# Where the state-space parameters keep their tables and operands: six tiles change their buffer pool, and one clearing is held back

## The chip, the cores and the metric

The program runs on one core of one Trainium2 chip (trn2). The metric is the device time of one execution in microseconds (us). The names used for the engines are PE (TensorE, matmul), PEld (its weight load), DVE (VectorE), ACT (ScalarE), POOL (GpSimd) and SP (SyncE, which here only issues DMAs).

## The reference

Four layers over 512 tokens of width 2048, in float32, and a norm behind the last. The first layer ("ab") is gated linear attention beside forgetting attention, the second ("c") a state-space layer, the third and fourth are a recurrent unit with window attention, and latent attention with differential attention. The change is in the parameters of the state-space layer, which depend on its weights alone. They are all that is shown:

```python
def s5_ssm(u, lam_re, lam_im, log_step, b_re, b_im, c_re, c_im, d):
    # groups of 16 channels share a 64-dim complex diagonal state:
    # x_t = Lbar x_(t-1) + Bbar u_t ; y_t = Re(C x_t) + D u_t
    lr = jnp.minimum(lam_re, -1e-4); li = lam_im
    step = jnp.exp(log_step)[:, None]
    mag = jnp.exp(lr * step)
    lb_re, lb_im = mag * jnp.cos(li * step), mag * jnp.sin(li * step)
    den = lr * lr + li * li
    nr, ni = lb_re - 1.0, lb_im
    coef_re = (nr * lr + ni * li) / den
    coef_im = (ni * lr - nr * li) / den
    bb_re = coef_re[..., None] * b_re - coef_im[..., None] * b_im
    bb_im = coef_re[..., None] * b_im + coef_im[..., None] * b_re
    ...                                   # scan over the tokens with Lbar, Bbar, C, D

def layer_c(x, ...):
    u, gate = split(rms_norm(x) @ w_in, 2)
    z = gelu(s5_ssm(u, ...))
    z = z * sigmoid(z @ glu_w + glu_b)
    return x + (z * silu(gate)) @ w_out
```

## The kernel before

Activations lie feature by feature: a tile is 128 features by 512 tokens. Every float32 factor of a large product is split into a high part and a rest (`split`: ACT rounds the high part, DVE subtracts it), and a product is three matmuls of 128x512 (high times high, high times rest, rest times high). Activations split this way are in tiles `hl`, weights in `whl`: a piece of weights comes by DMA into `wraw`, ACT writes its high part into `whl`, DVE the rest, and 12 matmuls then use it (`pj<-hl,whl` or `pj<-whl,hl`, all at line 152, where the one helper for matmuls stands; all two-operand elementwise work of DVE and POOL stands at line 140). There are four buffers of `whl` and three of `wraw`.

Tiles are taken from pools by tag (`self.t(tag, ...)`), with the number of buffers in `BUFS` (line 109): here `ha` 8, `hb` 3, `hc` 4, `vs` 4, `wk` 4, `wt` 2, `bc` 2, `rawa` 8, `rawb` 8; `cst`, `acc`, `acc2`, `fac` and `lm` have one. A new tile of a tag waits until the readers of the tile that had the buffer before are done. In PSUM, `pj` has four buffers, `sc` two, `tr` and `po` one each. A scheduler that simulates the program while it is built sets the order of the instructions in each engine's queue; on the chip each engine runs its queue strictly in that order and waits on semaphores. The order is thus fixed, and it depends on which buffer each tile has.

The parameters of layer c are worked out during layer ab and its output product, a piece at each of 21 places (`beside(o)` in the layer, `params(o)` in `emit`, o = 0 to 20):

- o = 0: `s5_params` (line 831), nearly all on POOL. It ends with two tables of powers, `Tb` (16 powers, 128x1024, two tiles of `vs`, lines 946 to 955) and `Ta` (8 powers, `hc`), and copies them by rows of four groups through `wt` into a table in device memory: 16 rows `s5tab` (lines 983 to 990), each by six copies on POOL and a DMA from POOL's queue. Before that a small table `s5w` goes out over `wrow` (`ha`, line 932).
- o = 1 to 8: `s5_tables(2(o-1))` (line 998) loads two rows of `s5tab` into `lm` and forms with DVE, for each of the two, a cosine and a sine table `C`, `Sn` of 128x512 (`hc`, line 1006), each from two products (`cst`, `acc`) and a sum. They go out by DMA (`s5ph`), issued by ACT's queue. I call one such cosine or sine table with its three DVE instructions a half-table; there are 32.
- o = 3 to 18: `s5_batch_params(o-3)` (line 1022), for batch b = 0 to 15: it loads `M`, `X1`, `Y` (two `vs` each), makes on POOL two outputs over `Z` (`cst`, line 1046) into `hc` and sends them out, on DVE the operand `GG` (`acc2`, line 1060) and on POOL the operand `BB` (`fac`, line 1072). At the next place follow PE's 32 small products of them (`tr<-vs,fac` and `tr<-acc,fac`, lines 1081 to 1086), and their result goes over `X3`, a part of `X1`, to device memory.

Layer ab in the stretch that matters: `fox(i)`, i = 0 to 3, is forgetting attention for two heads (scores `sc`, softmax by DVE and ACT, transposes into `tr`, copy to `pt`, products `po` with the value tiles, which lie in `vs`), and between them stand the projections of the next heads and the gates. The mixed output of the layer is in `rawa` and `rawb`, eight tiles each, `rawb` filling up from fox(0) to fox(3); `split_all` turns all sixteen into `hl` (`hl<-rawa,hl`, `hl<-rawb,hl`) at the start of `w_out`, the output product. Layer c later takes a tile `M0` per batch (`hb`, line 1099), cleared by POOL at line 1101; nothing there holds the clearing back until layer c.

## Time and profile before

| | |
|---|---|
| median of 3 runs | 3413.39 us (3410.92 to 3414.65) |
| the profiled execution | 3418.24 us, of which the span (first to last instruction) is 3416.4 us |
| PE busy | 3350.7 us, 98% of the span |
| DVE, ACT, POOL busy | 1907.5 us (56%), 1335.0 us (39%), 784.1 us (23%) |
| mean granted TensorE clock | 0.993 |

A row "`a<-b`" names the tile written and the tiles read, by the program's names. "[3.48 <-DVE whl L140]" behind a row of a timeline is the idle time of that engine just before it, and what ended it: the instruction of DVE at line 140 that wrote `whl`. PEclk is the TensorE clock that was granted in a stretch, as a share of full speed. Busy shares are means over the whole program; what counts for a change in one stage is who waits for whom in that stage.

### The profile page before, as it was taken

Reading aid. Unit: us, or ns where it says so; the run is one execution under the profiler, and the core shown is the slowest. Engines: PE = TensorE matmul, PEld = TensorE weight load, DVE = VectorE, ACT = ScalarE, POOL = GpSimd, SP = SyncE. Lnnn points to the kernel's source line nnn. Section 1 sums busy time; section 2 is a strip of 40 time slices with the busy share of each in tenths; the row PEclk is TensorE's granted clock in tenths of the full one; section 3 lists DMA queues with packets and bytes.
Section 4 is the critical chain, followed back from the end, with each engine's and each line's share of the span. In section 5 each row is a group of like instructions: output and inputs, shape, how many; then the busy total and the mean of one; then the engine's idle time right before and its main releaser. Section 6 shows DMA issues by size and latency. Waiting matters only on the chain.

```text
span 3416.4 us, 45778 instructions
## 1 busy us (share of the span) xinstructions
PE 3350.7 (98%) x16332; PEld 2719.7 (80%) x16332; DVE 1907.5 (56%) x3213; ACT 1335.0 (39%) x2497; POOL 784.1 (23%) x974
## 2 busy tenths in 40 slices
PE   8999998998999999999999999999999999999997
PEld 7888886776788888888888777888888788888885
DVE  5753457778455666834355656453544545647634
ACT  4442432233243333423343554232433444535522
POOL 0330365348612223300222010012110120212011
PEclk9999999999999999999999999999999999999999
DMA  5223335576634444343443223334333223232333
GB/s 149 75 69 90 89 99 168 165 217 196 203 121 131 137 144 136 119 120 119 144 127 90 71 72 87 96 120 142 107 90 83 72 65 83 79 90 73 107 118 107
DMA packets 389013, 390.01 MB, mean 114 GB/s; under 512 B 66968, under 2 KB 327448, under 8 KB 388784
## 3 DMA queue, kind: packets, MB, share of 16 engines
q1 hardware_dynamic: 362992, 354.64, 36.4%
q10 hardware_dynamic: 22464, 22.12, 1.9%
q0 software_dynamic: 3328, 10.32, 0.8%
q8 instruction: 128, 2.10, 0.3%
q14 instruction: 101, 0.83, 0.1%
HBM read 340.71 MB, written 46.25 MB: 113 GB/s over the span
## 4 chain that ended last, share of the span: by engine, by line
PE 89%; POOL 4%; DVE 3%; DMA 2%; issue 1%; ACT 1%; ACTq 0%; DVEq 0%; SPq 0%; POOLq 0%
PE pj L152 79%; PE sc L152 4%; PE po L152 3%; PE tr L156 2%; DMA s5tab<-wt 1%; POOL vs L140 1%; POOL hc L140 1%; PE tr L152 1%; POOL fac L140 1%; POOL cst L140 1%; POOL wt L140 0%; DVE whl L140 0%; DVE wk L140 0%; POOL wt L987 0%; POOL acc L140 0%
## 5 line engine op out<-in xcount | busy, mean ns | idle before, releaser
L152 PE MATMUL pj<-hl,whl 128*128 128x512 f32 x10224 | 2463.4, 398 | 16.8 <-DVE whl L140 8.8
L152 PEld LDWEIGHTS pj<-hl,whl 128*128 128x128 f32 x10224 | 1912.8, 189 | 462.6 <-DVE whl L140 11.4
L140 DVE TENSOR_TENSOR whl<-wraw,whl 128x512 fp32r<-128x512 f32 (+2 forms) x1064 | 806.3, 760 | 1091.4 <-ACT whl L137 1083.4
L137 ACT ACTIVATE whl<-wraw 128x512 fp32r<-128x512 f32 (+2 forms) x1064 | 661.1, 623 | 1367.0 <-PE pj L152 1098.1
L152 PE MATMUL pj<-whl,hl 128*128 128x512 f32 (+2 forms) x2112 | 463.5, 378 | 7.6 <-DVE ha L140 3.8
L152 PEld LDWEIGHTS pj<-whl,hl 128*128 128x128 f32 x2112 | 372.5, 189 | 84.9 <-DVE whl L140 4.6
L140 POOL TENSOR_TENSOR acc<-acc,wt 128x512 f32<-128x512 f32 x73 | 102.9, 1418 | 798.6 <-ACT wt L137 797.4
L137 ACT ACTIVATE wk<-sc,sm 128x256 f32<-128x256 f32 (+3 forms) x160 | 79.6, 501 | 90.1 <-DVE sm L148 86.6
L140 POOL TENSOR_TENSOR ha<-wk,ha 64x512 fp32r<-64x512 f32 x32 | 45.0, 1406 | 290.7 <-ACT ha L137 264.2
L140 POOL TENSOR_TENSOR wt<-wt,acc 64x508 f32<-64x508 f32 x32 | 63.8, 1994 | 181.5 <-DVE wt L140 125.8
L140 POOL TENSOR_TENSOR wt<-ha,wk 128x256 f32<-128x256 f32 x72 | 62.4, 894 | 133.0 <-PE pj L152 60.0
L152 PE MATMUL po<-pt,vs 128*128 128x128 f32 x560 | 79.9, 276 | 0.0
L152 PE MATMUL sc<-ha,ha 128*128 128x128 f32 (+1 forms) x224 | 71.7, 392 | 3.5 <-DVE ha L140 2.8
L152 PEld LDWEIGHTS po<-pt,vs 128*128 128x128 f32 x560 | 72.8, 192 | 2.8 <-ACT pt L137 0.4
L156 PE MATMUL tr<-ident,wk 128*128 128x128 f32 x416 | 71.4, 274 | 1.4 <-DVE pt L509 1.1
L137 ACT ACTIVATE pt<-tr 128x384 f32<-128x384 f32 (+3 forms) x96 | 46.7, 487 | 62.2 <-PE tr L156 60.3
L148 DVE TENSOR_SCALAR wk<-wk,sm 128x256 f32<-128x256 f32 (+3 forms) x160 | 65.0, 420 | 4.5
L156 PEld LDWEIGHTS tr<-ident,wk 128*128 128x128 f32 x416 | 52.0, 141 | 18.8 <-issue 3.4
L137 ACT ACTIVATE ge<-ge 128x512 f32<-128x512 f32 x64 | 40.3, 630 | 68.1 <-DVE ge L140 56.6
L140 POOL TENSOR_TENSOR fac<-wt,acc 128x512 fp32r<-128x512 f32 x8 | 10.8, 1352 | 244.2 <-ACT acc L137 130.4
L521 DVE TENSOR_REDUCE sm<-sc 128x1 f32<-128x128 f32 (+3 forms) x96 | 45.9, 487 | 34.1 <-PE sc L152 33.3
L140 POOL TENSOR_TENSOR cst<-vs,vs 128x256 f32<-128x256 f32 x64 | 54.0, 863 | 34.6 <-DMA vs<-s5w 27.2
(316 smaller groups left out, 2983.6 us busy)
## 6 DMA issues: line engine op xcount, KB each, us to landing
wraw<-in_l_w_in_dram SPq DMA_DIRECT2D x272, 256.0 KB, 2.8
wraw<-in_ab_w_in_dram SPq DMA_DIRECT2D x216, 256.0 KB, 2.8
wraw<-in_c_w_in_dram SPq DMA_DIRECT2D x128, 256.0 KB, 2.7
wraw<-in_l_w_out_dram SPq DMA_DIRECT2D x128, 256.0 KB, 2.9
wraw<-in_ab_w_out_dram SPq DMA_DIRECT2D x64, 256.0 KB, 3.3
wraw<-in_glu_w_dram SPq DMA_DIRECT2D x64, 256.0 KB, 3.0
wraw<-in_c_w_out_dram SPq DMA_DIRECT2D x64, 256.0 KB, 2.9
wraw<-in_l_w_in_dram SPq DMA_DIRECT2D x128, 128.0 KB, 2.3
```

The lines of the kernel that those rows point to most:

```text
L137: return self.nc.scalar.activation(out, in_, func, **kw)
L140: return (eng or self.nc.vector).tensor_tensor(out, a, b, op=op)
L148: return e.tensor_scalar(out, a, s1, None, op0=op0)
L152: return self.nc.tensor.matmul(out, l, r, start=start, stop=stop)
L156: return self.nc.tensor.transpose(out, in_, self.ident[:k, :k])
L521: self.nc.vector.tensor_reduce(mx, pb[:, 0:w], axis=AX.X, op=ALU.max)
```

## The change

- `wrow` goes from the pool `ha` into `lm`, which has one buffer.
- `Tb` goes from two tiles of `vs` into four halves in `rawb` (`Tb`, `Tb2`), so that a row of `s5tab` takes eight copies instead of six.
- `C` and `Sn` go from `hc` to `rawb`.
- `Z` goes from `cst` to `bc`.
- `GG` and `BB` of odd batches go to `hc`; those of even ones stay in `acc2` and `fac`.
- The clearing of `M0` is held behind the last instruction of that kind in the parameters (the clearing of `X3`, line 1087 before, 1090 after).

```diff
--- before.py
+++ after.py
@@ -929,7 +929,7 @@
                     s_ = 2 * half + j
                     o = (2 * i + j) * P
                     self.tr(pw_[0:64, o:o + P], N[8 + i] if s_ == 3 else W[:, i, s_])
-            wrow = self.t("ha", [64, 2, 2, P])
+            wrow = self.t("lm", [64, 2, 2, P])
             self.act(wrow.rearrange("p i j f -> p (i j f)"), pw_[0:64])
             for j in range(2):
                 for gg in range(2):
@@ -943,7 +943,8 @@
         cmul(c2, d2, co, si, co, si)
         cmul(N[11], N[12], c2, d2, c2, d2)
 
-        Tb = [self.t("vs", [P, 16, H]) for _ in range(2)]
+        half = lambda: self.hd("rawb").rearrange("p (n h) -> p n h", h=H)
+        Tb, Tb2 = [half(), half()], [half(), half()]
         Ta = [self.t("hc", [P, 8, H]) for _ in range(2)]
         tmp = [self.t(tag, [P, 8, H]) for tag in ("fac", "acc2")]
         tt_ = self.t("cst", [P, S])
@@ -960,12 +961,13 @@
 
                 pb_ = [p_.to_broadcast([P, m, H]) for p_ in pw]
                 u0, u1 = tmp[0][:, 0:m], tmp[1][:, 0:m]
+                to = Tb2 if m == 8 else [x[:, m:2 * m] for x in tab]
                 self.tt(u0, tab[0][:, 0:m], pb_[0], A.mult, eng=g)
                 self.tt(u1, tab[1][:, 0:m], pb_[1], A.mult, eng=g)
-                self.tt(tab[0][:, m:2 * m], u0, u1, A.subtract, eng=g)
+                self.tt(to[0], u0, u1, A.subtract, eng=g)
                 self.tt(u0, tab[0][:, 0:m], pb_[1], A.mult, eng=g)
                 self.tt(u1, tab[1][:, 0:m], pb_[0], A.mult, eng=g)
-                self.tt(tab[1][:, m:2 * m], u0, u1, A.add, eng=g)
+                self.tt(to[1], u0, u1, A.add, eng=g)
                 sq = [x[:, 0] for x in tmp]
                 self.tt(sq[0], pw[0][:, 0], pw[0][:, 0], A.mult, eng=g)
                 self.tt(sq[1], pw[1][:, 0], pw[1][:, 0], A.mult, eng=g)
@@ -983,7 +985,8 @@
             qs = slice(4 * b, 4 * b + 4)
             st = self.wk("wt")[:, 0:236]
             for i in range(2):
-                g.tensor_copy(st[:, i * 64:i * 64 + 64].rearrange("p (n q) -> p n q", q=4), Tb[i][:, :, qs])
+                for j, x in enumerate((Tb, Tb2)):
+                    g.tensor_copy(st[:, i * 64 + j * 32:i * 64 + j * 32 + 32].rearrange("p (n q) -> p n q", q=4), x[i][:, :, qs])
                 g.tensor_copy(st[:, 128 + i * 32:160 + i * 32].rearrange("p (n q) -> p n q", q=4), Ta[i][:, :, qs])
             g.tensor_copy(st[:, 192:196], M[:, 10, qs])
             g.tensor_copy(st[:, 196:236].rearrange("p (i q) -> p i q", q=4), M[:, 0:10, qs])
@@ -1003,7 +1006,7 @@
         for b in range(2):
             Tb = tab[:, b, 0:128].rearrange("p (i n q) -> p i n q", i=2, q=4)
             Ta = tab[:, b, 128:192].rearrange("p (i n q) -> p i n q", i=2, q=4)
-            C, Sn = self.hd("hc"), self.hd("hc")
+            C, Sn = self.hd("rawb"), self.hd("rawb")
             u = [self.t("cst", [P, S]), self.t("acc", [P, S])]
             v4 = lambda ap: ap.rearrange("p (q a b) -> p q a b", q=4, a=8)
             av = lambda i: Ta[:, i].rearrange("p n q -> p q n").unsqueeze(3).to_broadcast([P, 4, 8, 16])
@@ -1043,7 +1046,7 @@
 
         d = [self.dp.tile(sh, F32, name=self.name("s5d")) for sh in ([P, 2, 256], [P, 2, S], [4, P, 64])]
         self.s5d.append(d)
-        Z = self.t("cst", [P, S])
+        Z = self.t("bc", [P, S])
         z0, z1 = Z[:, 0:256], Z[:, 256:512]
         for i in range(2):
             o = self.hd("hc")
@@ -1057,7 +1060,7 @@
                         A.add if i else A.subtract, eng=g)
             g.dma_start(d[1][:, i], o)
 
-        GG = self.t("acc2", [P, 2, 256])
+        GG = self.t("hc" if b % 2 else "acc2", [P, 2, 256])
         v = lambda ap: ap.rearrange("p (q t c) -> p q t c", q=4, t=4)
         cb = lambda i: CP[:, i].unsqueeze(2).to_broadcast([P, 4, 4, 16])
         lb = lambda i: M[:, 0:32].rearrange("p (t i q) -> p i q t", t=4, i=2)[:, i].unsqueeze(3).to_broadcast([P, 4, 4, 16])
@@ -1069,7 +1072,7 @@
         self.tt(GG[:, 1], u1, u0, A.subtract)
         nc.scalar.dma_start(d[0], GG)
 
-        BB = self.t("fac", [P, 4, 4, 32])
+        BB = self.t("hc" if b % 2 else "fac", [P, 4, 4, 32])
         co = lambda i: M[:, 32 + 4 * i:36 + 4 * i].unsqueeze(2).to_broadcast([P, 4, 32])
         for i in range(2):
             self.tt(BB[:, 2], BP[:, 0], co(i), A.mult, eng=g)
@@ -1084,7 +1087,7 @@
         for i in range(2):
             for q in range(4):
                 self.mm(pt[rows(q), 16:64], BB[:, i, q], GG[:, i, q * 64:q * 64 + 48], start=(i == 0), stop=(i == 1))
-        g.memset(X3[:, 0:48], 0.0)
+        self.params_end = g.memset(X3[:, 0:48], 0.0)
         self.stt(X3[:, 48:64], self.own, self.c("s5_d", b), pt[:, 0:16], A.mult, A.add)
         self.act(X3[:, 64:112], pt[:, 16:64])
         for s_ in range(4):
@@ -1098,7 +1101,8 @@
         G, Br, Bi = [self.hd("ha") for _ in range(3)]
         M0 = self.t("hb", [P, 4, 2, 64])
         H = (slice(0, 64), slice(64, 128))
-        g.memset(M0, 0.0)
+        with self.after([self.params_end]):
+            g.memset(M0, 0.0)
         for i in range(2):
             self.dma.dma_start((Br, Bi)[i], d[1][:, i])
             self.dma.dma_start(G[H[i]].rearrange("p (g f) -> p g f", g=2), d[0][:, i].rearrange("(g p) f -> p g f", g=2))
```

The scheduler gives each queue a new order. Three places follow, each before and then after.

POOL, at the first power table. `vs_2975` and `vs_2948` hold the scalar parameters; `vs_3074` and `vs_3075` are `Tb` before, `rawb_3074` and `rawb_3075` its first halves after. Before:

```order
L140 TENSOR_TENSOR vs_2948<-vs_2948 128x64 x2
L140 TENSOR_TENSOR vs_2975<-vs_2948 128x64
L954 MEMSET vs_3074 128x64
L140 TENSOR_TENSOR fac_3078<-vs_3074,vs_2975 128x64
L955 MEMSET vs_3075 128x64
L140 TENSOR_TENSOR acc_3079<-vs_3075,vs_2975 128x64
L140 TENSOR_TENSOR vs_3074<-fac_3078,acc_3079 128x64
```

After:

```order
L140 TENSOR_TENSOR vs_2975<-vs_2948 128x64
L140 TENSOR_TENSOR vs_2948<-vs_2948 128x64 x2
L140 TENSOR_TENSOR fac_3080<-rawb_3074,vs_2975 128x64
L140 TENSOR_TENSOR vs_2975<-vs_2948 128x64
L140 TENSOR_TENSOR acc_3081<-rawb_3075,vs_2975 128x64
L1090 MEMSET vs_4286 128x48
L140 TENSOR_TENSOR rawb_3074<-fac_3080,acc_3081 128x64
```

Before, the clearing of `Tb`'s second tile (line 955) stands between the first two products. After, the clearings stand at the very start of POOL's queue, and the products follow the scalar work directly.

DVE, at the first half-table (`cst_3738` before, `cst_3772` after; `lm` are the rows loaded from `s5tab`). Before, it stands behind the second head pair's gates:

```order
L143 SCALAR_TENSOR_TENSOR rawa_2335<-ge_4436,rawa_2335 128x512
L140 TENSOR_TENSOR whl_4512<-wraw_4510,whl_4512 128x512
L140 TENSOR_TENSOR whl_4529<-wraw_4527,whl_4529 128x512
L140 TENSOR_TENSOR whl_4546<-wraw_4544,whl_4546 128x512
L140 TENSOR_TENSOR cst_3738<-lm_3734 128x512
L140 TENSOR_TENSOR acc_3739<-lm_3734 128x512
L140 TENSOR_TENSOR whl_4563<-wraw_4561,whl_4563 128x512
L140 TENSOR_TENSOR hc_3736<-cst_3738,acc_3739 128x512
```

After, it stands inside the projection ahead of fox(1), right behind the softmax of fox(0) (`wk_3743` is its last tile; `ha_3928` and `ha_3936` are projections for the next heads):

```order
L530 RECIPROCAL sm_3742<-sm_3742 128x1
L140 TENSOR_TENSOR ha_3928<-pj_3796,bc_230 128x512
L148 TENSOR_SCALAR wk_3743<-wk_3743,sm_3742 128x512
L140 TENSOR_TENSOR cst_3772<-lm_3768 128x512
L140 TENSOR_TENSOR acc_3773<-lm_3768 128x512
L140 TENSOR_TENSOR ha_3936<-pj_3797,bc_230 128x512
L140 TENSOR_TENSOR whl_3993<-wraw_3991,whl_3993 128x512
L140 TENSOR_TENSOR whl_4010<-wraw_4008,whl_4010 128x512
```

Two `whl` tiles that PE needs stand directly behind the first two products of the table.

DVE, where the mixed output is split at the start of the output product. Before, only splits, weights and operands of the batches stand there:

```order
L140 TENSOR_TENSOR hl_7080<-rawb_3658,hl_7080 128x512
L140 TENSOR_TENSOR hl_7083<-rawb_3732,hl_7083 128x512
L140 TENSOR_TENSOR hl_7086<-rawb_4146,hl_7086 128x512
L140 TENSOR_TENSOR whl_7126<-wraw_7124,whl_7126 128x512
L140 TENSOR_TENSOR hl_7089<-rawb_4220,hl_7089 128x512
L140 TENSOR_TENSOR hl_7092<-rawb_5174,hl_7092 128x512
L140 TENSOR_TENSOR whl_7143<-wraw_7141,whl_7143 128x512
L140 TENSOR_TENSOR hl_7095<-rawb_5248,hl_7095 128x512
```

After, half-tables of the batches 12 to 15 (`lm_6050`, then `lm_6142`) stand among them:

```order
L140 TENSOR_TENSOR hl_7114<-rawb_3692,hl_7114 128x512
L140 TENSOR_TENSOR whl_7143<-wraw_7141,whl_7143 128x512
L140 TENSOR_TENSOR hl_7117<-rawb_3766,hl_7117 128x512
L140 TENSOR_TENSOR rawb_6052<-cst_6054,acc_6055 128x512
L140 TENSOR_TENSOR hl_7120<-rawb_4180,hl_7120 128x512
L140 TENSOR_TENSOR whl_7160<-wraw_7158,whl_7160 128x512
L140 TENSOR_TENSOR hl_7123<-rawb_4254,hl_7123 128x512
L140 TENSOR_TENSOR cst_6054<-lm_6050 128x512
L140 TENSOR_TENSOR acc_6055<-lm_6050 128x512
```

Eight half-tables, less the first two products, stand from here on within the next 66 rows of DVE's queue; before, all of them stood ahead of the splits, in the stretch of fox(3). Their buffers `rawb` are those of the mixed output, and come free as its tiles are split.

## Rows read from the trace of the kernel before

**Rows 1.** The page: engines' busy time, and the chain that ended last.

```profile
PE 3350.7 (98%) x16332; PEld 2719.7 (80%) x16332; DVE 1907.5 (56%) x3213; ACT 1335.0 (39%) x2497; POOL 784.1 (23%) x974
...
PE 89%; POOL 4%; DVE 3%; DMA 2%; issue 1%; ACT 1%; ACTq 0%; DVEq 0%; SPq 0%; POOLq 0%
```

**Rows 2.** Windows: stretch, length, busy us of each engine (instructions), PEclk, DMA.

```profile
432.00:497.00 65.00, 65.00 (x318) 52.66 (x317) 34.26 (x72) 21.76 (x48) 43.14 (x89) 1.00 0.32 85
...
497.00:560.00 63.00, 50.67 (x209) 39.03 (x208) 51.15 (x63) 10.26 (x18) 49.58 (x103) 0.89 0.58 172
...
670.00:705.00 35.00, 31.49 (x165) 23.69 (x164) 30.18 (x63) 10.23 (x26) 21.30 (x30) 0.95 0.80 220
...
755.00:822.00 67.00, 55.20 (x327) 41.93 (x326) 55.98 (x77) 23.07 (x47) 55.78 (x85) 0.92 0.60 180
...
765.00:825.00 60.00, 48.20 (x305) 36.23 (x304) 53.12 (x71) 20.75 (x42) 50.51 (x76) 0.91 0.56 169
```

**Rows 3.** Waits of PE between 480 and 860 us: total, times, longest.

```profile
PE tr L152 <- POOL fac L140: 10.5, 5, 5.5
...
PE pj L152 <- DVE whl L140: 9.8, 7, 3.5
```

**Rows 4.** Waits of POOL and DVE between 300 and 900 us.

```profile
POOL vs L955 <- PE po L152: 65.6, 1, 65.6
...
POOL fac L140 <- PE tr L152: 46.6, 3, 23.6
...
DVE cst L140 <- DMA lm<-s5tab: 10.4, 3, 5.6
```

**Rows 5.** Timeline of POOL: start, us, engine, line, operation, tiles, [idle before].

```profile
382.34 0.76 POOL L140 TENSOR_TENSOR fac<-vs,vs 128x64 f32<-128x64 f32 x1
...
448.72 0.15 POOL L955 MEMSET vs<- 128x64 f32 x1 [65.62 <-PE po L152]
...
491.04 1.34 POOL L990 DMA_DIRECT2D s5tab<-wt  x2
```

**Rows 6.** Timeline of DVE.

```profile
424.03 0.69 DVE L140 TENSOR_TENSOR ha<-pj,bc 128x512 f32<-128x512 f32 x1 [0.21 <-PE pj L152]
...
424.74 0.69 DVE L140 TENSOR_TENSOR whl<-wraw,whl 128x512 fp32r<-128x512 f32 x1
...
497.27 1.07 DVE L140 TENSOR_TENSOR cst<-lm 128x512 f32<-128x512 f32 x1 [5.60 <-DMA lm<-s5tab]
```

**Rows 7.** Timeline of PE, a stretch without waits.

```profile
437.11 5.14 PE L152 MATMUL pj<-hl,whl 128*128 128x512 f32 x21
```

**Rows 8.** Groups of DVE, 497 to 552 us: count, busy us, mean ns, idle before.

```profile
L140 DVE TENSOR_TENSOR cst<-lm 128x512 f32<-128x512 f32 x12 | 13.4, 1119 | 10.4 <-DMA lm<-s5tab 10.4
...
L140 DVE TENSOR_TENSOR whl<-wraw,whl 128x512 fp32r<-128x512 f32 x12 | 9.1, 755 | 0.0
...
L140 DVE TENSOR_TENSOR hc<-cst,acc 128x512 f32<-128x512 f32 x12 | 8.6, 719 | 0.3
...
L140 DVE TENSOR_TENSOR vs<-vs,smb 128x256 f32<-128x256 f32 x2 | 0.8, 441 | 3.8 <-POOL wt L986 3.8
```

**Rows 9.** Timeline of POOL: the same copy beside an idle and a busy DVE.

```profile
494.25 0.24 POOL L986 COPY wt<-vs 128x64 f32<-128x64 f32 x1 [1.87 <-DMA s5tab<-wt]
...
539.32 1.08 POOL L986 COPY wt<-vs 128x64 f32<-128x64 f32 x1
```

**Rows 10.** Timeline: small products of batches 3 and 5, and what lies between.

```profile
735.63 0.32 PE L152 MATMUL tr<-vs,fac 128*32 128x16 f32 x16
...
745.74 1.43 POOL L140 TENSOR_TENSOR cst<-vs,vs 128x256 f32<-128x256 f32 x2 [5.78 <-DMA vs<-s5w]
...
750.93 0.26 PE L152 MATMUL tr<-vs,fac 128*32 128x16 f32 x8
```

**Rows 11.** Groups of POOL, 755 to 822 us: two of these per batch.

```profile
L1050 POOL MEMSET hc<- 128x512 f32 x9 | 4.7, 526 | 1.9 <-DMA s5d<-hc 1.5
```

**Rows 12.** Groups of DVE, 765 to 825 us.

```profile
L140 DVE TENSOR_TENSOR whl<-wraw,whl 128x512 fp32r<-128x512 f32 x17 | 20.2, 1194 | 3.8 <-ACT whl L137 3.6
```

## The prediction, made before the changed kernel ran

> **What bounds the kernel now.** I read the page's totals and chain first: PE is busy 98% of the span and makes up 89% of the chain that ended last [rows 1], so only what lets PE stand still, or run at less than full clock, can be won. The windows show where that is: three stretches only, with PE busy to the full between them. From 497 to 560 us PE stands for 12.3 of 63 us at a granted clock of 0.89; from 670 to 705 for 3.5 of 35 at 0.95; from 765 to 825 for 11.8 of 60 at 0.91 [rows 2]. That is 27.6 us of idle time. Counting what is missing to full clock over the whole of a stretch as lost (63 x 0.11 + 35 x 0.05 + 60 x 0.09 = 14.1 us), all that can be won there is 41.7 us. All three lie in the stretch in which the parameters of layer c are made.
>
> The waits name the partners [rows 3]: POOL's operand `fac` for the small products (10.5 us in five waits) and DVE's rests of the weights (9.8 in seven). One step further back [rows 4], POOL waited once for 65.6 us at line 955, the clearing of `Tb`'s second tile, for PE's products `po` that read the value tiles in the pool `vs`, and three times, 46.6 us in all, before it could write `fac`, for the small products that read the `fac` before. DVE waited 10.4 us for the table rows.
>
> **Part 1: `Tb` in `rawb`, and what it moves.** The wait at line 955 stands between the first product of the table, at 382.34, and the rest; from the clearing at 448.72 to the first rows leaving at 491.04 POOL needs 42.3 us [rows 5]. Without the wait the rows leave at about 383.1 + 42.3 = 425.4 us, 65.6 us earlier. Before, the first half-table started 6.2 us behind the issue [rows 5, 6]; that gives 431.6 us, and 432.5 with the two extra copies in each of the first two rows, at 0.24 us. The change puts the first half-table behind work that DVE reached at 424.0 [rows 6]. So DVE stands some 8 us, and the weights behind it come late: three DVE instructions (2 x 1.12 for the products, 0.69 for `ha`) and the rest of the weights itself, 0.69, give 432.5 + 3.6 = 436.1 instead of 425.4, 10.7 us late. What covers that are the `whl` buffers: 12 matmuls each at 5.14/21 = 0.245 us [rows 7] are 2.9 us, and three buffers ahead of the one in use are 8.8. PE stands for the other 1.9 us (0 to 4).
>
> Then eight half-tables run beside fox(1). Each costs DVE two products of 1.12 and a sum of 0.72, 2.96 us [rows 8]; eight are 23.7, and the six small instructions of the first `GG`, at 0.44, 2.7. From 432 to 497 DVE was busy for 34.3 us [rows 2]; with these it is 60.7 of 65, 93%. PE's transposes there need the softmax from DVE, through one PSUM buffer. A step that falls at random into a half-table waits half of it, 1.5 us; eight times that is 12, none is 0; I take 6, since projections can fill the other half. With 1 us for what is left of the old stretch from 505 to 560 (0 to 3: of its twelve half-tables eight have gone ahead), and 2 us of clock (0 to 4), the first stretch costs 1.9 + 6 + 1 + 2 = 10.9 instead of 12.3 + 6.9 = 19.2. Bounds: 0 and 23.
>
> The rows of `s5tab` take eight copies now, and they move beside a DVE that is at work. There the same copy took 1.08 us instead of 0.24 [rows 9], and DVE paid little: the rests of the weights had a mean of 0.755 us there [rows 8], beside 0.69 alone [rows 6]. I charge nothing: the next rows are wanted 25 us later.
>
> The Trainium skill speaks against this move ("SBUF — State Buffer", section "Who interferes with whom"): a DVE instruction with two inputs in SBUF and a GpSimd instruction that reads SBUF share a port pair, and whichever starts first holds it for its whole instruction. Row and rule agree as to POOL (its copy has the length of the DVE product beside it). By the rule DVE might pay as well, and by it the first stretch would move toward its upper bound; the measured 0.755 says that here mostly POOL pays.
>
> **Part 2: `C` and `Sn` in `rawb`.** They no longer take turns in `hc` with POOL's outputs. The price is in the order: `rawb` holds the mixed output, which is full by fox(3), and so the eight half-tables of the batches 12 to 15 go from before fox(3)'s end to behind the splits at the start of the output product. They leave the second stretch, from 670 to 705, where DVE was busy for 30.2 of 35 us [rows 2] and PE lost 3.5 + 1.7 = 5.2 us; I leave 2 of these (0 to 5.2). They arrive where DVE was busy for 53.1 of 60 us [rows 2] and the rest of one piece of weights took 1.194 us in the mean [rows 12], beside POOL at work for 50.5 of 60. At that share some 70 us would hold 62 us of DVE's old work, and 22 of their 24 instructions add 7 x 2.96 + 0.72, about 21.4: 83 us in 70. The lead of the weights takes 8.8 of the 13 us too many. I take 4 us (0, if the rests fall back to 0.69, which would free 17 x 0.5 = 8.6; up to 16, if nothing of the lead is there, with 3 of clock).
>
> **Part 3: two buffers for `GG` and `BB`, `Z` in `bc`.** The three waits of POOL, 46.6 us, go: an odd batch's `BB` need not wait for the even one's products. Those to the batches 1 and 2 lay beside a busy PE, so the wait itself gives nothing; it lets the operands be ready ahead. What stays are `X1` and `Y` in `vs`, two batches deep: batch 5 loads when batch 3's result is out. Between the small product of batch 3 and that of 5 lay 15.3 us (735.63 to 750.93), 10 of these until POOL could start on batch 5's data [rows 10]. In the changed order of PE 48 large matmuls stand between them, 11.8 us at 0.245: PE waits 3.5 us. POOL needs 55.8 us for nine half batches (two clearings each) [rows 2, 11], 12.4 us per batch. Between the products of 5 and 6 stand 22 matmuls, 5.4 us; batch 6 waits at least 1 us (its data come 15.3 us behind batch 4's product, which stands 26 matmuls behind batch 3's) and at most 7 (POOL's 12.4); I take 4. Then 58 and 63 matmuls stand between products, 14.2 us and more, over 12.4; I put 2 us on batch 7. That is 9.5 us of idle and 4 of clock, 13.5 instead of 11.8 + 5.4 = 17.2. Bounds: 7 and 21.
>
> **Part 4: the rest.** The clearing of `M0` leaves POOL's queue between the batches and goes behind the last of them; who needs it, layer c, comes behind the whole output product. `wrow` in one buffer makes the second half wait for the first half's DMAs, on ACT, which is ahead of PE there. Both at nothing (0 to 2).
>
> **Sum.** Lost before: 19.2 + 5.2 + 17.2 = 41.6. Lost after: 10.9 + 2 + 4 + 13.5 = 30.4. The gain is 11.2 us. The profiled execution took 3418.24 us, which gives 3407.0; it stands 4.85 us above the median of 3413.39, so the median I expect is 3402.2, said as 3402. A difference below 0.2%, 6.8 us, can't be told from none for this kernel.
>
> **The rivals.**
>
> *All of it goes.* The tables are ready so early that DVE's surplus is absorbed, and the two sets of operands break the chain of the small products; only the lower bound of part 3 is left, 7 us, in all a gain of 34.6: 3379. For it: the 65.6 us are real and so is the room (DVE 34.3 of 65). Against it: batches 5 and 6 still hang on `X1`. With gains over 20 us its chance is 0.20.
>
> *The loss only moves.* POOL's chain keeps pace with nothing (the operands were not what was late, the loads of `X1` and the 12.4 us per batch were), so that the third stretch stays at 17.2, and fox(1) pays what fox(2)'s projections paid before: 19.2 + 2 + 4 + 17.2 = 42.4, or 3414; within 6.8 us of 3413. In this case the change doesn't do what it says for the small products. Chance 0.19.
>
> *DVE is too full at the start of the output product.* One mechanism, on the other side: the eight late half-tables stand in DVE's queue ahead of weights and splits, while POOL's work on the batches slows DVE to 1.194 us per rest. If all 21 rests of that stretch take that, and the lead is used up by batch 6's wait, the 13 us too many and the 8.6 that were hoped back come on PE, 21.6, and 5 of clock: 26.6 in place of 4. With the rest as forecast 22.6 more than 3402: 3425, slower than before. It decides from about 15 us on in place of 4 (even) and 22 (slower by more than the bound). Chance 0.17.
>
> **How the numbers follow.** Forecast (gains of 7 to 20 us): 0.44, with a range of its own from 3393 to 3407. With the rivals, faster by over 0.2% has 0.44 + 0.20 = 0.64, no difference 0.19, slower 0.17. The range for 8 in 10 runs from all of it (3379) to near the slow case: 3380 to 3422.
>
> **What would show it.** In the profile after: line 956 without a wait and the first `s5tab` issue near 425; DVE waiting some 8 us for `lm` near 424 to 432 and PE under 4 there; short waits of PE for `tr<-ident,wk` or `po` between 450 and 500; no wait of PE of over 3 us from 505 to 550; waits of 3 to 7 us before the small products of batches 5 and 6; POOL's waits for `fac` gone. Wrong would be: new idle time of PE behind `whl` or `hl` at the start of the output product of over 10 us, or PE's old waits at the small products unchanged.

## The result, and the profile after

The changed kernel is slower: 3444.67 us (3443.44 to 3446.1, 4 runs) against 3413.66 us, a ratio of 1.0093 with a 95% interval of 1.0082 to 1.0105, or 31 us. I had forecast 3402, with 3422 as the upper end. Its profiled execution has a span of 3442.1 us, 25.7 us more than that of before. The profiled execution of before, at 3418.24 us, stands 4.6 us above the median of its runs, so what its profile shows of this kernel is a little long.

The windows of the kernel after, over the stretch of the parameters (columns as in [rows 2]):

```profile
380.00:505.00 125.00, 120.03 (x553) 93.73 (x553) 85.78 (x171) 39.61 (x89) 98.17 (x228) 0.99 0.47 134
505.00:640.00 135.00, 135.00 (x685) 108.84 (x685) 74.42 (x134) 41.73 (x85) 16.51 (x29) 1.00 0.43 123
640.00:710.00 70.00, 58.51 (x272) 44.62 (x271) 54.71 (x97) 17.58 (x41) 38.19 (x49) 0.90 0.64 190
710.00:825.00 115.00, 101.97 (x605) 79.19 (x603) 85.73 (x118) 35.71 (x70) 67.42 (x98) 0.94 0.57 168
825.00:945.00 120.00, 105.59 (x571) 80.13 (x571) 60.40 (x96) 27.07 (x52) 87.74 (x115) 0.96 0.64 201
```

The same of the kernel before:

```profile
380.00:505.00 125.00, 125.00 (x604) 100.75 (x602) 67.07 (x146) 42.49 (x92) 52.56 (x106) 1.00 0.35 94
505.00:640.00 135.00, 122.67 (x564) 96.65 (x563) 96.52 (x157) 36.75 (x79) 57.27 (x118) 0.95 0.55 161
640.00:710.00 70.00, 66.49 (x355) 52.34 (x354) 56.42 (x103) 18.11 (x41) 33.47 (x49) 0.98 0.69 198
710.00:825.00 115.00, 103.16 (x648) 80.65 (x647) 91.77 (x132) 40.26 (x81) 73.77 (x115) 0.96 0.64 191
825.00:945.00 120.00, 120.00 (x662) 95.50 (x661) 66.16 (x93) 34.29 (x65) 82.30 (x115) 1.00 0.69 219
```

Between 380 and 640 us the change does what it says: 5 us of PE idle in place of 12.3. Then it loses 11.5 us from 640 to 710 (3.5 before) and, above all, 14.4 from 825 to 945, where the kernel before loses nothing. DVE is not busier there than before (60.4 us against 66.2).

The small products are milestones. Counted in the traces, those of the batches 0, 2, 10 and 15 stand behind the same number of large matmuls in every kernel here (2208, 2496, 3072 and 3552 from the start; e11 and e12 differ at batch 10). Those of the batches 3 to 9 do not: batch 8's stands behind 2921 before and 2898 after, 23 matmuls or 5.6 us earlier. Three of them in the kernel after (batches 0, 2 and 15), then in the kernel before:

```profile
582.49 0.36 PE L152 MATMUL tr<-acc,fac 128*32 128x48 f32 x16
...
670.61 0.53 PE L152 MATMUL tr<-acc,fac 128*32 128x48 f32 x16
...
987.10 0.36 PE L152 MATMUL tr<-hc,hc 128*32 128x48 f32 x16
```

```profile
592.78 0.36 PE L152 MATMUL tr<-acc,fac 128*32 128x48 f32 x16
...
672.81 0.36 PE L152 MATMUL tr<-acc,fac 128*32 128x48 f32 x16
...
961.60 0.36 PE L152 MATMUL tr<-acc,fac 128*32 128x48 f32 x16
```

The kernel after is 10.3 us ahead at batch 0, 2.2 at batch 2, and 25.5 behind at batch 15; behind that the two run alike. The waits of DVE from 790 to 960 us say what has changed, after and before:

```profile
DVE whl L140 <- ACT whl L137: 29.5, 21, 3.8
DVE hc L140 <- DMA s5d<-hc: 11.2, 2, 6.9
DVE smb L148 <- POOL fac L140: 8.8, 1, 8.8
DVE vs L140 <- POOL bc L140: 6.7, 1, 6.7
DVE vs L140 <- DMA vs<-in_s_bc_dram: 5.1, 1, 5.1
```

```profile
DVE whl L140 <- ACT whl L137: 61.4, 28, 4.9
DVE hl L140 <- ACT hl L137: 2.5, 2, 1.8
```

Before, DVE waited for weights, that is, it was ahead. After, it stands for the data of the batches, with weights behind it in its queue. The timeline of the kernel after shows one such case whole:

```profile
820.60 13.67 POOL L140 TENSOR_TENSOR bc<-vs,vs 128x256 f32<-128x256 f32 x2 [4.00 <-DMA vs<-s5w]
...
832.24 0.74 DVE L140 TENSOR_TENSOR whl<-wraw,whl 128x512 fp32r<-128x512 f32 x1
...
835.01 0.34 SPq L1033 DMA_DIRECT2D smb<-s5tab  x1
...
839.65 1.29 DVE L140 TENSOR_TENSOR vs<-vs,smb 128x256 f32<-128x256 f32 x2 [6.67 <-POOL bc L140]
...
840.86 1.21 DVE L140 TENSOR_TENSOR rawb<-cst,acc 128x512 f32<-128x512 f32 x1
...
842.10 0.33 ACTq L1022 DMA_DIRECT2D s5ph<-rawb  x1
842.55 1.15 ACT L137 ACTIVATE whl<-wraw 128x512 fp32r<-128x512 f32 x2 [13.27 <-DVE rawb L140]
...
843.23 2.08 PE L152 MATMUL pj<-hl,whl 128*128 128x512 f32 x4 [5.67 <-ACT whl L137]
```

DVE comes to the operand of the next batch before POOL has read that batch's tile, and stands 6.67 us. Behind it stands the sum of a late half-table; ACT has this table's DMA issue next in its queue and stands 13.27 us with the next weights behind it; PE stands 5.67. None of these three is overloaded: each queue is in order and holds something too early.

POOL is late here for a reason of its own, the 13.67 us of the first row. The chain that ended last, 790 to 990 us, runs through it and through the next such row; its longest pieces, but for PE's, are

```profile
820.60 13.67 POOL bc L140 x2
846.13 6.90 POOL bc L140 x2
```

PE's large matmuls make up 29.3% of that chain, 89.2% before. How much of the loss is due to these two slow rows no run parts; they are not needed for a loss, since e1 below has no such row of over 3 us there and still loses 4.3 us from batch 10 to 15.

### The profile page after: what moved, and what is told of

Read it like the earlier page. It is cut to its first block, busy times and chain, and to the rows that moved or that the text cites. A ratio compares the mean times of both kernels' runs of the same rounds, so it can differ in the third digit from the quotient of the medians.

```text
span 3442.1 us, 45827 instructions
## 1 busy us (share of the span) xinstructions
PE 3360.0 (98%) x16332; PEld 2721.5 (79%) x16332; DVE 1903.0 (55%) x3213; ACT 1335.8 (39%) x2497; POOL 801.9 (23%) x1006
## 4 chain that ended last, share of the span: by engine, by line
PE 86%; DVE 5%; POOL 5%; DMA 2%; issue 2%; ACT 0%; DVEq 0%; ACTq 0%; SPq 0%; POOLq 0%
PE pj L152 76%; PE sc L152 4%; PE po L152 3%; PE tr L156 1%; POOL bc L140 1%; POOL hc L140 1%; POOL wt L140 1%; DVE whl L140 1%; POOL vs L140 1%; DVE acc L140 1%; DVE wk L140 1%; PE tr L152 1%; POOL fac L140 0%; DMA vs<-s5w 0%; DMA s5d<-hc 0%
## 5 line engine op out<-in xcount | busy, mean ns | idle before, releaser
L140 POOL TENSOR_TENSOR bc<-vs,vs 128x256 f32<-128x256 f32 x64 | 71.9, 1145 | 54.2 <-DMA vs<-s5w 43.5
L140 POOL TENSOR_TENSOR fac<-wt,acc 128x512 fp32r<-128x512 f32 x8 | 10.8, 1354 | 244.3 <-ACT acc L137 130.3
```

Of the source, the lines that this page charges most:

```text
L140: return (eng or self.nc.vector).tensor_tensor(out, a, b, op=op)
```

## The experiments

All edits are on the kernel named; `cs` stands for the pool of `C` and `Sn`. The table gives the milestones of each profile, worked out from the first product `128x48` of a batch: batch 0's time, and the times on to the batches 2, 10 and 15. DVE is the sum of its waits for other things than ACT's weights, 790 to 960 us. Each ratio is to runs of the kernel before made beside that run (their medians lie between 3409.65 and 3414.49 us), so differences of medians and of ratios are not quite the same. In e11 and e12 batch 10's product stands some 45 large matmuls (11 us) later in PE's order: there the last two stretches can't be compared with the other rows.

| run | median us | ratio to before, interval | b0 | b0 to b2 | b2 to b10 | b10 to b15 | DVE |
|---|---|---|---|---|---|---|---|
| before | 3413.66 | 1 | 592.8 | 80.0 | 173.6 | 115.2 | 8 |
| after | 3444.67 | 1.0093, 1.0082 to 1.0105 | 582.5 | 88.1 | 190.5 | 126.0 | 37 |
| e1 | 3441.40 | 1.0089, 1.0074 to 1.0104 | 598.9 | 84.2 | 181.4 | 119.5 | 38 |
| e2 | 3424.04 | 1.0039, 1.0024 to 1.0054 | 586.0 | 83.2 | 186.7 | 114.7 | 3 |
| e3 | 3453.58 | 1.0126, 1.0111 to 1.0141 | 596.4 | 82.2 | 193.2 | 124.8 | 38 |
| e4 | 3428.66 | 1.0053, 1.0036 to 1.0069 | 603.5 | 80.5 | 173.1 | 115.2 | 5 |
| e5 | 3421.90 | 1.0029, 1.0016 to 1.0041 | 593.3 | 80.1 | 177.7 | 115.4 | 37 |
| e6 | 3437.94 | 1.0078, 1.0063 to 1.0093 | 593.5 | 82.6 | 182.9 | 123.5 | 19 |
| e7 | 3421.37 | 1.0028, 1.0016 to 1.0039 | 599.1 | 80.1 | 172.2 | 115.2 | 6 |
| e8 | 3416.60 | 1.0014, 1.0005 to 1.0024 | 584.3 | 84.0 | 179.3 | 115.2 | 9 |
| e9 | 3433.06 | 1.0055, 1.0040 to 1.0070 | 588.8 | 83.3 | 183.8 | 119.3 | 11 |
| e10 | 3422.06 | 1.0027, 1.0018 to 1.0036 | 586.6 | 84.5 | 174.0 | 117.2 | 6 |
| e11 | 3413.80 | 1.0006, 0.9997 to 1.0016 | 586.5 | 81.2 | 178.4 | 110.3 | 5 |
| e12 | 3424.65 | 1.0033, 1.0022 to 1.0044 | 587.3 | 83.3 | 190.5 | 107.2 | 10 |
| e13 | 3427.37 | 1.0041, 1.0026 to 1.0056 | 590.9 | 81.9 | 181.6 | 114.7 | 5 |
| e14 | 3421.90 | 1.0025, 1.0015 to 1.0034 | 591.5 | 82.6 | 174.0 | 115.2 | 5 |
| e15 | 3421.30 | 1.0023, 1.0013 to 1.0032 | 586.7 | 88.5 | 176.0 | 115.2 | 4 |
| e16 | 3419.32 | 1.0019, 1.0009 to 1.0028 | 584.2 | 87.4 | 175.0 | 114.7 | 4 |
| e17 | 3429.89 | 1.0046, 1.0033 to 1.0060 | 586.9 | 82.5 | 192.1 | 115.2 | 9 |
| e18 | 3413.41 | 0.9997, 0.9988 to 1.0006 | 586.9 | 85.8 | 169.0 | 115.2 | 9 |

**Taking parts back from the changed kernel (e1 to e4).** e1:

```diff
-            C, Sn = self.hd("rawb"), self.hd("rawb")
+            C, Sn = self.hd("hc"), self.hd("hc")
```

> The changed kernel with C and Sn back in the pool hc, everything else as changed. By the order the tables of the batches 12 to 15 stand ahead of the splits again (none behind the first hl), and the first half-table stands a little earlier still. Theory A (the eight half-tables behind the splits make DVE too full at the start of the output product, and DVE, POOL, ACT and SP then wait for each other in a ring): the loss from 800 to 945 us of the changed kernel goes, about 30 us, and the 10 us won by 582 us stay: 3400 to 3412 us. Theory B (GG and BB of odd batches in hc: POOL's outputs wait for PE's small products): nothing of the loss goes, and with C and Sn in hc as well the waits for hc grow: 3440 to 3460 us.

e2:

```diff
-        GG = self.t("hc" if b % 2 else "acc2", [P, 2, 256])
+        GG = self.t("acc2", [P, 2, 256])
-        BB = self.t("hc" if b % 2 else "fac", [P, 4, 4, 32])
+        BB = self.t("fac", [P, 4, 4, 32])
```

> The changed kernel with GG and BB of odd batches back in acc2 and fac, everything else as changed; the half-tables stay where the change put them, eight of them behind the splits. Theory A: the loss at the start of the output product stays, 3435 to 3455 us. Theory B: POOL's waits for hc on PE's small products (34.7 and 28.9 us in the changed kernel) go, and most of the 31 us with them: 3405 to 3420 us.

e3 (the copies and the doubling go back with it):

```diff
-        Tb, Tb2 = [half(), half()], [half(), half()]
+        Tb = [self.t("vs", [P, 16, H]) for _ in range(2)]
```

> The changed kernel with Tb back in vs (six copies per row), everything else as changed. Both theories: the 10.3 us that the changed kernel was ahead at batch 0's small products (582.4 against 592.7) go, and the loss at the start of the output product stays: 3450 to 3460 us. If Tb were itself the cause of the loss, the time would fall to about 3415.

e4 is e1 and e2 together.

> The changed kernel with C and Sn back in hc and GG and BB back in acc2 and fac; Tb in rawb, Z in bc, wrow in lm and the held clearing stay. By the order this has ten half-tables less in fox(3)'s stretch: they stand earlier. Theory A: as e1 or a few us better, 3395 to 3408 us, since nothing but the tables moves earlier. Theory B: 3400 to 3412 us too; it tells A from B only beside e1 and e2.

Theory A alone falls with e1: 15.6 us come back behind batch 2, but 16.4 are lost by batch 0, since more half-tables now stand in fox(0). e2 gives back 18 us by the ratios; its DVE no longer stands for the batches:

```profile
DVE whl L140 <- ACT whl L137: 46.7, 21, 5.9
DVE smb L140 <- ACT smb L137: 1.5, 1, 1.5
```

From batch 2 to 10, e4 needs 13.6 us less than e2. e8, below, has none of the half-tables behind the splits and needs 7.4 less than e2; the rest goes with the tables of the batches 0 to 11 (e8 to e4). e4 as a whole missed both theories, by the 603.5 of its batch 0. e3 shows that `Tb` was the part that won: without it batch 0 comes at 596.4.

**One part alone, and the parts told apart (e5 to e8).** e5 and e7 are the kernel before with the edit of `GG` and `BB`, and of `Tb`, alone. e6, which also holds the clearing of `M0` back:

```diff
-        GG = self.t("acc2", [P, 2, 256])
+        GG = self.t("hb" if b % 2 else "acc2", [P, 2, 256])
-        BB = self.t("fac", [P, 4, 4, 32])
+        BB = self.t("bc" if b % 2 else "fac", [P, 4, 4, 32])
```

> The kernel before with GG and BB of odd batches in hc and nothing else changed. Its half-tables stand where those of before stand, to within one weight tile. Theory B, as the runs so far have it (in hc the operands and POOL's two outputs per batch take turns in four buffers, and POOL and DVE wait for PE's small products and for the outputs' DMAs): the stretch from batch 8's to batch 15's product grows from 153 us to about 168, and the time by 12 to 20 us, to 3422 to 3431 us. Theory C (the loss of the operands comes about only together with the half-tables in rawb): no change, 3407 to 3415 us.

> The kernel before with the second buffer of GG in hb and that of BB in bc, and the clearing of M0 held back (it uses hb); nothing is in hc that was not there before. Theory B: it is hc and not the second buffer that costs; the waits of POOL for fac go and nothing takes their place, 3400 to 3411 us. If a second buffer as such cost time (batches further ahead, POOL and DVE in each other's way), it would be as slow as e5.

> The kernel before with Tb in rawb (eight copies per row) and nothing else. By the order the half-tables stand as far ahead as in e4, 20 weight tiles ahead of where they stood. Theory D (with Tb free the half-tables come so early that they fall into fox(0) and fox(1), where DVE and POOL are then full, and the gain turns into a loss): batch 0's products at about 603 us instead of 592.8, as in e4, and no loss later: 3418 to 3430 us. If e4's early loss came from Z in bc, wrow in lm or the held clearing, this is faster than before, 3398 to 3408 us.

e8, on e2:

```diff
-            C, Sn = self.hd("rawb"), self.hd("rawb")
+            cs = "rawb" if b0 < 12 else "hc"
+            C, Sn = self.hd(cs), self.hd(cs)
```

> The changed kernel with C and Sn of the batches 12 to 15 in hc (those of 0 to 11 in rawb as changed), and GG and BB back in acc2 and fac. By the order the early half-tables stand as in the changed kernel, and none behind the splits. If the parts add up: e2's 3424 us less the 10 us that e2 lost between the products of batches 8 and 10, so about 3413 us (3406 to 3418), with batch 0's products at 582 to 586 us. If the eight late half-tables cost nothing, 3420 to 3428 us.

e6 fells theory B as it was put: the second operands cost more outside `hc` than in it. So it is not `hc` alone; that it is the second buffer, and not the other users of `hb` and `bc`, is shown only by e13, for the stretch behind batch 10. `Tb` alone (e7) loses 6.3 us by batch 0: the early half-tables are a gain only where `rawb` keeps them from coming still earlier. PE's window in e7, against 125.0 before:

```profile
380.00:505.00 125.00, 110.83 (x488) 85.56 (x486) 88.53 (x166) 32.17 (x73) 102.39 (x233) 0.94 0.46 131
```

e8 adds up as expected: 7.4 us under e2 (8.5 by the ratios), the price of the late half-tables, and 0.14% over before.

**Loads off SP (e9 to e12).** On the changed kernel, e6, the kernel before and e8:

```diff
-        self.dma.dma_start(M, self.s5tab[b][:, 196:236])
+        g.dma_start(M, self.s5tab[b][:, 196:236])
...
-        self.dma.dma_start(X1[:, 0:896], I["s5_bc"][b])
-        self.dma.dma_start(Y[:, 0:512],
+        g.dma_start(X1[:, 0:896], I["s5_bc"][b])
+        g.dma_start(Y[:, 0:512],
```

> The changed kernel with the three loads of each batch (M, X1, Y) issued from POOL's queue in place of SP's; SP then brings weights and table rows without standing behind a load that waits for a buffer. Half-tables and small products stand nearly as in the changed kernel. Theory E (with second operand buffers the loads of the batches stand up to nine weight tiles further ahead in SP's queue, wait there for their buffers, and hold the weights back): ACT's waits for wraw of the output product (34.4 us between 790 and 960 in the changed kernel, 2.5 before) mostly go, and the time falls by 15 to 25 us, to 3418 to 3430 us; the rest is the eight late half-tables. Theory F (the ring of POOL, DVE and ACT alone, by waits for hc, slow POOL instructions and ACT's blocked queue): 3438 to 3452 us.

> e6 (second GG in hb, second BB in bc, clearing held) with the loads M, X1, Y on POOL's queue. Theory E: the 9.5 us that e6 was ahead of the kernel before at batch 8's product stay, and the 30 us lost behind it go: 3402 to 3414 us. Theory F: as e6, 3430 to 3442 us.

> Control: the kernel before with M, X1, Y on POOL's queue and nothing else. The loads then wait behind POOL's own work, and each costs POOL an issue of about 0.6 us (the s5tab issues took 0.54 to 0.58), 48 in all, 29 us of POOL. Both theories: about as before, 3410 to 3422 us, since before lost nothing to loads on SP in the output product; a gain of more than 5 us would say that SP held weights back before, too.

> e8 (C and Sn of the batches 12 to 15 in hc, one buffer each for GG and BB, the rest as changed) with M, X1, Y on POOL's queue. e8 lost 11 us of PE between 640 and 710 us, more than the kernel before (3.5), while SP stood before Y and X1. Theory E: part of that comes back, 3405 to 3414 us. Theory F: 3413 to 3422 us.

Both two-buffer kernels win (11.6 and 15.9 us), the control stays, e12 loses 8. e9 and e10 lie between what the two theories gave, e12 above both. Theory E's sign is missing: ACT's wait for `wraw` does not mostly go. It is 26.5 us in e9 (34.4 in the changed kernel), and in e10 (31.3 in e6):

```profile
ACT whl L137 <- DMA wraw<-in_ab_w_out_dram: 33.9, 22, 3.3
```

e5 has 33.4 us of it as well, and loses nothing behind batch 10. So this wait doesn't tell what costs. What fell in e9 and e10 are DVE's waits for the batches (37 to 11, 19 to 6). As it was put, E is not borne out; but the two gains stand, so where the loads stand is not ruled out as a part of the loss. These runs also moved DVE's operand work: its first instruction of the batches 13 to 15 has 261, 266 and 273 weight tiles ahead of it in e9, 254, 261 and 269 in the changed kernel. That, and what POOL's issues cost and save, can't be taken apart.

**Holding DVE's operand work (e13 to e18).** e13, on e6, and e17, on the changed kernel (`self.x3` is the instruction of DVE that reads the products of the batch before):

```diff
-        self.tt(v(u0), cb(0), lb(0), A.mult)
-        self.tt(v(u1), cb(1), lb(1), A.mult)
+        with self.after([self.x3] if self.x3 is not None else []):
+            self.tt(v(u0), cb(0), lb(0), A.mult)
+            self.tt(v(u1), cb(1), lb(1), A.mult)
```

> e6 (second GG in hb, second BB in bc) with DVE's first two instructions for GG held behind the result of the batch before (the instruction of DVE that reads the small products), so that DVE's queue has them no earlier than one buffer would allow; the buffers and POOL's part stay two deep. Theory G (the second buffer lets the scheduler put DVE's operand work six to seven weight tiles further ahead, DVE comes to it before its data are there, stands, and the weights behind it are late): DVE's waits for other things than weights between 790 and 960 us fall from 19 to under 8 us, batch 8 to batch 15 takes 153 to 162 us instead of 183.5, and the time is 3408 to 3420 us. Theory E (the loads on SP alone): the loads stand as in e6 and the loss stays, 3430 to 3442 us.

> The changed kernel with DVE's first two instructions for GG held behind the result of the batch before, as in e13; nothing else. Theory G, as e13 has left it (operands two deep let DVE's queue run ahead of the batches' data; that costs behind batch 9's product, 156.4 us to batch 15's against 138.2 before): batch 9 to batch 15 takes 136 to 142 us, and the time is 3422 to 3434 us; the eight late half-tables and what is given back between batches 8 and 9 stay. If the late half-tables alone make the loss there: 3438 to 3448 us.

e14 is e6 with the second buffers for `b < 8` alone, e15 is e8 with the changed kernel's second buffers for `b < 8`, e16 is e15 with `rawb` for `b0 < 8`, and e18 is e8 with `rawb` for `b0 < 8`.

> e6 with the second buffers for the batches 1, 3, 5, 7 alone; from batch 9 on one buffer each, as before. The order to batch 8 is e6's, behind it that of the kernel before. Theories E and G: the 9.5 us that e6 was ahead at batch 8's product stay for the most part, and behind it nothing is lost: 3402 to 3412 us. If the loss of e6 came from what stands before batch 8 (POOL and DVE behind by then): 3420 to 3438 us.

> e8 (C and Sn of 12 to 15 in hc, Tb, Z, wrow and the held clearing as changed) with the changed kernel's second buffers of GG and BB in hc for the batches 1, 3, 5, 7 alone. If the parts add up: e8's 3416.6 us less the 6 to 10 us that two buffers won between the products of batches 2 and 8: 3406 to 3411 us. If hc is too full for it (four half-tables, two outputs and two operands in four buffers): 3416 to 3428 us.

> e15 with C and Sn in rawb for the batches 0 to 7 alone, those of 8 to 15 in hc: the half-tables of 8 to 11, which stand packed at the end of fox(2) in the changed kernel, where it lost 8 us between the products of batches 1 and 2, start ten weight tiles earlier. If that packing is the loss: 3398 to 3406 us, faster than before. If it is the batches' loads and outputs there: as e15, 3406 to 3414 us.

> The kernel that the parts point to: Tb in rawb, C and Sn in rawb for the batches 0 to 7 and in hc for 8 to 15, one buffer each for GG and BB, Z, wrow and the held clearing as changed. From e8 and e4: batch 0's product at 584 us (before 592.8), 80 to 82 us on to batch 2's, since by the order the half-tables of 8 to 15 stand spread out as in e4, and 288 us from there to batch 15's, as in every run with one buffer and no late half-tables (before 288.8, e4 288.2, e8 294.4): 6 to 10 us faster than before, 3403 to 3408 us. If the stretch to batch 15 takes e8's 294: 3410 to 3414 us.

With the hold, the five batches from 10 to 15 take 114.7 and 115.2 us, PE's own pace (114.7 to 115.2 in every kernel in which PE doesn't wait there), and the changed kernel gets 14.8 us back (16 by the ratios) with all its buffers kept. DVE's waits in e17, 790 to 960 us:

```profile
DVE whl L140 <- ACT whl L137: 41.4, 24, 4.1
DVE whl L140 <- DMA hb<-s5d: 3.3, 1, 3.3
DVE vs L143 <- PE tr L152: 2.5, 1, 2.5
```

So it is the order that the second buffers bring, and not the buffers, that costs behind batch 10: shown in both kernels. That it is DVE's queue, as theory G has it, is not shown apart from E. The expectation of e13 took the loads to stay where they were, and they did not: with the hold the last batch's `Y` has 311 pieces of weights ahead of it in SP's queue in e13 and e17, as before, and 304 in e6 and the changed kernel. DVE's operand work of that batch moved from 269 to 283 tiles, further than its 276 before. No run moves one of the two queues alone.

Nor is it all. e13 missed its 3420, since from batch 2 to 10 it stays as slow as e6 (181.6 and 182.9; 173.6 before), and e17 takes 192.1 there. e5 stands as long as the changed kernel (37 us), and of the 4.9 us that it loses by batch 15 hardly any lie behind batch 10: standing by itself need not cost. That it costs only where the lead of the weights is gone already is a reading, not shown.

e14 came out where its expectation had put a loss from before batch 8. Its batch 8 product comes at 798.7 (808.4 before), as in e6, and I had taken that for a gain. But it stands 41 large matmuls, 10 us, earlier in PE's order. From batch 2 to 10 PE stands for 15.4 us, 15.3 before: the second buffers of the early batches win nothing there. e15 came out in its slower range and e16 above both of its ranges; with e18 they show that parts don't add. e18's profile is 4.6 us ahead at batch 15, no more than the profile of before is over its median; its own median is 1.1 us under before, with an interval that holds 1. No kernel here beats the one before by a measurable amount.

## Why the prediction was wrong

**Part 1 was right in size, and for less than I thought.** The wait at line 955 went; the rows left at 424.5 (forecast 425.4), and the first half-table started at 431.94 (forecast 432.5), DVE standing 3.3 us, not 8, because it came there later itself:

```profile
431.94 1.08 DVE L140 TENSOR_TENSOR cst<-lm 128x512 f32<-128x512 f32 x1 [3.28 <-DMA lm<-s5tab]
```

PE did not stand there; from 380 to 505 us it stood for 5.0 us in all, at the softmax, where my terms had 8.9. Batch 0 came 10.3 us earlier, against 8.3 in my term (19.2 less 10.9). But the early start wins only together with `C` and `Sn` in `rawb` (e7, e4).

**The second stretch failed.** I left 2 of its 5.2 us, and PE stood for 11.5 us from 640 to 710, 3.5 before. More than half is one wait, just behind batch 2's product, the longest of the whole program but one: with eight half-tables packed at the end of fox(2), DVE writes `ha` late. After, then before:

```profile
PE sc L152 <- DVE ha L140: 6.6, 1, 6.6
```

```profile
PE sc L152 <- DVE ha L140: 2.8, 1, 2.8
```

I had counted only the half-tables that leave from 670 to 705, not those that the new order packs ahead of them. The wait is 6.2 to 8.6 us in e2, e8 and e15, which pack them as well, and 2.9 and 3.3 in e16 and e18, where those of the batches 8 to 11 start earlier. The other 4.9 us are waits for weights ahead of batch 2's product, a part of the 8.1 us that the changed kernel takes longer from batch 0 to 2. These the packing does not explain, since e16 and e18 still take 87.4 and 85.8 us there; with one operand buffer (e2) or the hold (e17) it is 83.2 and 82.5. Why is open.

**Part 2 was mis-sized.** Half-tables behind the splits: 4 us forecast, 7.4 measured in the time (e2 less e8, 8.5 by the ratios), and as much between the batches 2 and 10 of the profiles. The mechanism was not the one I named: DVE was busy for half of the time from 825 to 945 us, and rests took 0.86 us in the mean from 800 to 945. What cost, in the one case shown above, was ACT's queue behind a table's DMA issue.

**Part 3 failed, and with it the sign.** "It lets the operands be ready ahead" came true at the small products: from 672 to 810 us PE's waits for `fac` fell from 10.5 to 1.9 us, where I had put 9.5. But its waits for weights grew by nearly as much. After, then before:

```profile
PE pj L152 <- DVE whl L140: 8.4, 3, 5.0
PE tr L152 <- POOL fac L140: 1.9, 2, 1.2
```

```profile
PE tr L152 <- POOL fac L140: 10.5, 5, 5.5
PE pj L152 <- DVE whl L140: 1.3, 2, 0.8
```

So nothing was won: from batch 2's product to batch 8's PE stood for 15.7 us, 15.3 before. The sum ended there. I let the stretch behind 825 us stand at zero because the kernel before has no idle time in it. But an operand buffer more is also leave to put the batch's work earlier in the queues. By the order, DVE's first operand instruction of the batches 13, 14 and 15 has 254, 261 and 269 weight tiles ahead of it in the changed kernel, in e5 and in e6, and 260, 268 and 276 before and in e2: six or seven tiles earlier with two buffers, and ahead of its data. The loads on SP moved with it. I had asked of each wait what is behind it, and of this added room nothing. Behind batch 10 the changed kernel loses 10.8 us by it. The time falls by 14.8 us where the work is held back (16 by the ratios, e17), and by 18 where the buffers go (e2).

By the ratios the 31 us are 18 for the second operand buffers (after to e2), 8.5 for the late half-tables (e2 to e8) and 4.8 for the rest (e8); by the intervals each is good to some 5 us only. The slower rival had the right place, and a wrong reason: not a DVE too full, but a DVE that stands.

## What to carry to other kernels

Where a scheduler orders in-order queues at build time, a second buffer is also leave to put work earlier in a queue that others share; ask which queue stands, and what is behind, when the data come later than the scheduler believed. Add the buffer and hold the order separately, and measure both; and see which other queues the hold moves. A milestone compares two kernels only where the same work stands ahead of it. A stretch without idle time before is a stretch to be priced: it can only get worse.

## What the runs showed of the hardware

Two multiplications on POOL that take 1.44 us together elsewhere in the same profile (at 762.34) took 13.67 us from 820.60, while DVE ran without a pause until 832.98, mostly on two-input instructions; POOL's ended at 834.27, 1.3 us after DVE had stopped. The Trainium skill ("SBUF — State Buffer", "Who interferes with whom") has whichever engine comes second wait for the first one's instruction; here POOL seems to have waited over a row of them. Spans on POOL are rough, and no run here isolates it.
